# Layer 0 of a three-layer block: gates one branch later, modulation weights by GpSimd's queue, four places for gated z

## The chip, the cores and the metric

One core of a Trainium2 chip. The time is that of the device for one execution, in microseconds, as the median of three runs. The profile shown is of one further execution.

## The reference

The program computes a stack of three layers on x (1024 positions, 1024 channels, float32) with a conditioning vector c. Before each of the first two layers c gives a shift, a scale and a gate by a 1024 x 3072 matrix (the modulation); h is the normed x, scaled and shifted; the layer's output is multiplied by the gate and added to x. The change lies in layer 0, a recurrent block:

```python
proj = h @ in_w
xb, zg = proj[..., :D_RNN], proj[..., D_RNN:]
xb = causal_dwconv(xb, conv_w) + conv_b
pre = jnp.einsum('bsni,knij->kbsnj', xg, gate_w.astype(jnp.float32))   # xg: xb in 8 blocks of 128 channels
gates = jax.nn.sigmoid(pre)                                            # with gate_b
r_t, i_t = gates[0], gates[1]
log_a = -RG_C * r_t * jax.nn.softplus(-lam.astype(jnp.float32))
a_t = jnp.exp(log_a)
mult = jnp.sqrt(-jnp.expm1(2.0 * log_a))
b_t = mult * (i_t * xf)
_, hseq = lax.associative_scan(_lin_combine, (a_t, b_t), axis=1)
y = hseq.astype(h.dtype) * jax.nn.silu(zg)
return y @ out_w
```

Layer 1 is a gated delta rule in chunks, layer 2 a mix of a long convolution and a state-space model. Neither is touched.

## The kernel before, in words

Channels lie on the 128 partitions, positions along the free axis. The 1024 channels of layer 0 are worked in four groups p of 256 (two blocks e of 128). Weights come from memory in pieces of 1 MB (tile wst, two places), and are split into two float16 parts wh and wl (L104 by ScalarE, L105 by VectorE, four places); a product is three matmuls (L111 to L113), eight steps of 128 for each half of 512 positions, so 24 matmuls for one PSUM bank psmm. A group has an input branch and a z branch.

- xbranch(p): shift_proj (32 narrow matmuls for the shift's part), four projections into banks that ScalarE copies to xp (L323), the convolution of four taps (L329 by ScalarE, three L331 by VectorE for each block) into xf. Then the gates: eight float32 matmuls of xf with the gate matrices gw (L512) into banks ps_gate, sigmoids by ScalarE (L513) into gt0 and gt1, a tanh (L519) and an exponential (L522), VectorE's arithmetic (L523, L524, L527, L528) with ScalarE's L525 and square root L526 in between, and two scans (L531) that give the hidden state hs. gt0, gt1 and at have one place each. xf has one place for even and one for odd groups.
- zbranch(p): four projections, each read by ScalarE with the SiLU (L542) into zs, multiplied by the hidden state (L543), and split into two float16 parts (L123, L125) that lie over the hidden state and go into the output projection.

Beside that the modulation of later use is worked out in six parts: ada_fetch loads four tiles ast of 512 KB (four places, 24 loads in all), ada_sum multiplies them by c and adds up (L148, seven L150 for each part, VectorE), and ada_fin adds over the partitions (four transposes on TensorE, ps_ada, L186 and L187) and writes 512 numbers to memory (ada_d, L189) from GpSimd's queue. ada_step does one of each, a stage further for each part. The next stage reads ada_d back as rows GA, hn and SH.

All engines take their instructions in order. A scheduler orders them when the program is built, from the order in which the code is written and from places and data; waits between engines are semaphores. Within layer 0 the parts stand one after the other in the code at the end of the listing, with ada_step between them. SyncE's queue carries all loads of layer 0; GpSimd carries the memsets of xp's first three columns (L313), the six writes of ada_d, and later the writes of x1_d (tile x_d in the views).

Of the kernel before, what the change touches and what calls it, by code (L numbers as in the profile page):

```python
# [10 lines left out]
F32 = mybir.dt.float32  # L11
# [6 lines left out]
P = 128  # L18
D = 1024
# [5 lines left out]
WC = 256  # L25
# [3 lines left out]
def kernel(ctx, tc, ins, out):  # L29
    nc = tc.nc  # L30
    pe, dve, act, pool, sp = nc.tensor, nc.vector, nc.scalar, nc.gpsimd, nc.sync
    a = ins
# [123 lines left out]
    def ada_fetch(pl, l, part, h):  # L156

        tiles = []
        for kk in range(4):
            st = pl.tile([P, 2, 512], F32, tag="ast", name="ast", bufs=4)  # L160
            sp.dma_start(st, ada_src(l, part, h, 2 * kk, 2))
            tiles.append(st)
        return tiles, l, part, h

# [307 lines left out]
    with ExitStack() as sy:  # L472
        ypool = mkpool("y0", stack=sy)
        yT = []
        with ExitStack() as s0:
            pl = mkpool("lru", stack=s0)
            hseq = []
            PR = [P, 2, T]
            gw = []
            for g2 in range(2):  # L480
                g_ = pl.tile([P, D], F32, name=f"gw{g2}")
                sp.dma_start(g_.rearrange("p (n j) -> p n j", n=NK), a["lru_gate_w"][0, g2].rearrange("n i j -> i n j"))
                gw.append(g_)

            def xbranch(p, w):
                xf = xf0 if p == 0 else lru_xf(p, pl)
                if p > 0:
                    sb = shift_proj(w)
                for e in range(2 if p > 0 else 0):
                    xp = lru_xp(p, pl)  # L490
                    for hf in range(2):
                        lru_proj(xp, w, e, hf, sb[e])
                    lru_conv(xf[:, e], xp, 2 * p + e)
                if p == 0:
                    sb = shift_proj(w)
                    for e in range(2):
                        cs = pl.tile([P, 4], F32, tag="cs", name="cs", bufs=2)
                        dve.tensor_copy(cs[:, 0:1], col("lconv", e, 3))
                        for i in range(1, 4):
                            dve.tensor_tensor(out=cs[:, i:i + 1], in0=cs[:, i - 1:i], in1=col("lconv", e, 3 - i), op=ALU.add)  # L500
                        dve.tensor_scalar(out=cs, in0=cs, scalar1=sb[e], scalar2=None, op0=ALU.mult)
                        dve.tensor_tensor(out=xf[:, e, 0:3], in0=xf[:, e, 0:3], in1=cs[:, 0:3], op=ALU.add)
                        act.activation(xf[:, e, 3:], xf[:, e, 3:], AF.Identity, bias=cs[:, 3:4])
                tg = []
                for g2 in range(2):
                    gx = pl.tile(PR, F32, tag=f"gt{g2}", name=f"gt{g2}")
                    for e in range(2):
                        j = 2 * p + e
                        js = slice(P * j, P * (j + 1))
                        for hf in range(2):  # L510
                            ps = ps_c("ps_gate")
                            pe.matmul(ps, gw[g2][:, js], xf[:, e, HF[hf]], start=True, stop=True)  # L512
                            act.activation(gx[:, e, HF[hf]], ps, AF.Sigmoid, bias=col("lgb", j, g2))  # L513
                    tg.append(gx)
                at, it = tg
                tt = pl.tile(PR, F32, tag="at", name="at")
                for e in range(2):
                    j = 2 * p + e
                    act.activation(tt[:, e], at[:, e], AF.Tanh, scale=sp4[:, j:j + 1])  # L519
                for e in range(2):  # L520
                    j = 2 * p + e
                    act.activation(at[:, e], at[:, e], AF.Exp, scale=sp8[:, j:j + 1])  # L522
                dve.tensor_tensor(out=it, in0=it, in1=xf, op=ALU.mult)  # L523
                dve.scalar_tensor_tensor(out=at, in0=at, scalar=1.0, in1=tt, op0=ALU.add, op1=ALU.mult)  # L524
                act.activation(at, at, AF.Identity, bias=onecol)  # L525
                act.activation(tt, tt, AF.Sqrt, scale=-1.0)  # L526
                dve.scalar_tensor_tensor(out=tt, in0=at, scalar=1.0, in1=tt, op0=ALU.add, op1=ALU.mult)  # L527
                dve.tensor_tensor(out=tt, in0=tt, in1=it, op=ALU.mult)  # L528
                hs = ypool.tile(PR, F32, tag="a4", name="hs", bufs=4)
                for e in range(2):  # L530
                    dve.tensor_tensor_scan(hs[:, e], at[:, e], tt[:, e], 0.0, ALU.mult, ALU.add)  # L531
                hseq.append(hs)

            def zbranch(p, w):
                sb = shift_proj(w)
                for e in range(2):
                    yT.append([])
                    for hf in range(2):
                        ps = ps_mm()
                        mm_chT(ps, w, P * e, hTh(HF[hf]), hTl(HF[hf]))  # L540
                        zs = pl.tile([P, 512], F32, tag="zs", name="zs", bufs=2)
                        act.activation(zs, ps, AF.Silu, scale=IWS, bias=sb[e])  # L542
                        dve.tensor_tensor(out=zs, in0=zs, in1=hseq[p][:, e, HF[hf]], op=ALU.mult)  # L543

                        y = hseq[p][:, e, HF[hf]].bitcast(F16)
                        yT[-1].append((y[:, :512], y[:, 512:]))
                        split(y[:, :512], y[:, 512:], zs)

            adq = [(l, part, h) for l, part in ((0, 2), (1, 1), (1, 0)) for h in range(2)]
            adt, adp = [ada_fetch(pl, *adq.pop(0))], []  # L550

            def ada_step():
                if len(adp) == 2 or not adt:
                    ada_fin(pl, *adp.pop(0))
                if adt:
                    adp.append(ada_sum(pl, *adt.pop(0)))
                if adq:
                    adt.append(ada_fetch(pl, *adq.pop(0)))

            wx.append(load_w(a["lru_in_w"][0], 2 * WC))  # L560
            xbranch(0, wx[0])
            wz.append(load_w(a["lru_in_w"][0], D + WC))
            xbranch(1, wx[1])
            ada_step()
            wx.append(load_w(a["lru_in_w"][0], 3 * WC))
            zbranch(0, wz[0])
            ada_step()
            xbranch(2, wx[2])
            wz.append(load_w(a["lru_in_w"][0], D + 2 * WC))
            ada_step()  # L570
            zbranch(1, wz[1])
            wz.append(load_w(a["lru_in_w"][0], D + 3 * WC))
            ada_step()
            ada_step()
            xbranch(3, wx[3])
            ada_step()
            ada_step()
            zbranch(2, wz[2])
            ada_step()
            zbranch(3, wz[3])  # L580
# [972 lines left out]
```

## Time and profile before

| | |
|---|---|
| runs, median (lowest to highest) | 1833.15 us (1831.11 to 1836.46), 3 runs |
| profiled execution, its own time | 1828.97 us |
| its span | 1827.3 us |
| TensorE busy | 1741.6 us (95%) |
| VectorE busy | 1386.6 us (76%) |
| ScalarE busy | 920.1 us (50%) |
| GpSimd busy | 62.1 us (3%) |
| mean granted clock of TensorE | 0.989 |

The shares are of the whole span. Layer 0's part that the change touches lies between about 75 and 272 us; what it is worth there is read from that stretch alone. In the page a granted clock of 1.00 is TensorE's full clock. Names as psmm or ast stand for all places of a tile; L12 is line 12 of the listing.

### The profile page before, as it was taken

What the parts mean: (1) busy time and instruction counts of PE and PEld (TensorE: products, weight loads), DVE (VectorE), ACT (ScalarE), POOL (GpSimd) and SP (SyncE); (2) the same over time, 40 slices, a digit from 0 to 9 for tenths busy, and PEclk for the clock granted to TensorE, in tenths of its full rate; (3) what the DMA queues carried; (4) which work ended last, traced back from release to release, by engine and by line L of the source; (5) the groups of instructions that cost most, each with busy time, mean ns of one, the idle gap of its engine ahead of it and who ended that gap; (6) DMA issues with size and microseconds to landing.
All of it is one profiled execution on the core that took longest, in us unless ns stands there. A gap on an engine that the chain in (4) does not pass through costs nothing.

```text
span 1827.3 us, 28998 instructions
## 1 busy us (share of the span) xinstructions
PE 1741.6 (95%) x11591; PEld 1072.6 (59%) x11591; DVE 1386.6 (76%) x2429; ACT 920.1 (50%) x1642; POOL 62.1 (3%) x152
## 2 busy tenths in 40 slices
PE   4978999999899999999999998999999999999998
PEld 2433449855556656678789586555444444444487
DVE  6697767656777777887466799999999999693332
ACT  6576663256556857766443434655651221571221
POOL 0000000000000010100000300000000000000000
PEclk8999999999999999999999999999999999999999
DMA  9554345314142231444342311101321221011212
GB/s 305 164 157 140 57 72 190 104 55 132 30 120 69 62 79 33 113 130 117 128 150 82 89 50 52 53 20 51 127 81 35 70 69 64 30 41 52 81 70 93
DMA packets 165169, 165.23 MB, mean 90 GB/s; under 512 B 50094, under 2 KB 143342, under 8 KB 165034
## 3 DMA queue, kind: packets, MB, share of 16 engines
q1 hardware_dynamic: 163626, 159.17, 29.0%
q0 software_dynamic: 1408, 4.21, 0.6%
q8 instruction: 91, 1.49, 0.3%
q14 instruction: 44, 0.36, 0.1%
HBM read 139.05 MB, written 23.12 MB: 89 GB/s over the span
## 4 chain that ended last, share of the span: by engine, by line
PE 61%; DVE 25%; ACT 6%; issue 4%; DMA 3%; SPq 0%; DVEq 0%; ACTq 0%
DVE cc L1024 5%; PE psmm L113 5%; PE psmm L111 5%; PE psmm L112 5%; DVE wl L105 2%; PE ps_out L120 2%; PE ps_out L118 2%; PE ps_out L119 2%; PE ps_fin L120 2%; PE ps_fin L118 2%; PE ps_fin L119 2%; PE ps_zc L111 2%; PE ps_zc L113 2%; PE ps_zc L112 2%; ACT jk L728 1%
## 5 line engine op out<-in xcount | busy, mean ns | idle before, releaser
L111 PE MATMUL psmm<-hTh,wh 128*128 128x512 f16 x896 | 342.2, 383 | 12.7 <-ACT zs L542 10.2
L112 PE MATMUL psmm<-hTl,wh 128*128 128x512 f16 x896 | 342.8, 383 | 0.1
L113 PE MATMUL psmm<-hTh,wl 128*128 128x512 f16 x896 | 342.8, 383 | 0.0
L1024 DVE SCALAR_TENSOR_TENSOR cc<-cu,cols,cc 128x1024 f32<-128x1024 f32 (+1 forms) x270 | 301.2, 1160 | 0.9
L112 PEld LDWEIGHTS <-wh 128*128 128x128 f16 x1568 | 154.2, 98 | 183.6 <-issue 18.7
L113 PEld LDWEIGHTS <-wl 128*128 128x128 f16 x1568 | 154.2, 98 | 175.0 <-issue 8.3
L111 PEld LDWEIGHTS <-wh 128*128 128x128 f16 x1568 | 154.2, 98 | 174.4 <-issue 8.2
L105 DVE SCALAR_TENSOR_TENSOR wl<-wst,wh 128x2048 f16<-128x2048 f32 (+2 forms) x71 | 153.6, 2168 | 51.7 <-ACT wh L104 51.7
L104 ACT ACTIVATE wh<-wst 128x2048 f16<-128x2048 f32 (+2 forms) x71 | 128.4, 1811 | 94.0 <-PE ps_gs L112 27.7
L118 PE MATMUL ps_z<-wh,hTh 128*128 128x256 f16 x256 | 69.8, 273 | 0.0
L120 PE MATMUL ps_z<-wl,hTh 128*128 128x256 f16 x256 | 69.8, 273 | 0.0
L119 PE MATMUL ps_z<-wh,hTl 128*128 128x256 f16 x256 | 69.8, 273 | 0.0
L118 PE MATMUL ps_fin<-wh,merged 128*128 128x256 f16 x256 | 69.8, 273 | 0.0
L119 PE MATMUL ps_fin<-wh,merged 128*128 128x256 f16 x256 | 69.8, 273 | 0.0
L120 PE MATMUL ps_fin<-wl,merged 128*128 128x256 f16 x256 | 69.8, 273 | 0.0
L119 PE MATMUL ps_out<-wh,hs 128*128 128x256 f16 x256 | 69.7, 273 | 0.0
L118 PE MATMUL ps_out<-wh,hs 128*128 128x256 f16 x256 | 69.7, 273 | 0.0
L120 PE MATMUL ps_out<-wl,hs 128*128 128x256 f16 x256 | 69.7, 273 | 0.0
L123 ACT ACTIVATE hTh<-ps_ht 128x512 f16<-128x512 f32 x32 | 17.4, 595 | 88.0 <-PE ps_ht L271 88.0
L793 DVE TENSOR_TENSOR Tt<-Tt,tm 128x60 f32<-128x60 f32 (+24 forms) x248 | 55.9, 225 | 5.5
L791 DVE TENSOR_TENSOR tm<-Lp,Tt 128x60 f32<-128x60 f32 (+24 forms) x248 | 53.6, 216 | 5.2
L120 PE MATMUL ps_out<-wl,yo 128*128 128x256 f16 x192 | 52.3, 273 | 0.3 <-DVE wl L105 0.3
(531 smaller groups left out, 3999.9 us busy)
## 6 DMA issues: line engine op xcount, KB each, us to landing
wst<-in_w_in_dram SPq DMA_DIRECT2D x24, 1024.0 KB
wst<-in_gdn_in_w_dram SPq DMA_DIRECT2D x16, 1024.0 KB
ast<-in_ada_w_dram SPq DMA_DIRECT2D x24, 512.0 KB
xt<-in_x_dram SPq DMA_DIRECT2D x16, 512.0 KB
wst<-in_lru_in_w_dram SPq DMA_DIRECT2D x8, 1024.0 KB
sta<-in_ada_w_dram SPq DMA_DIRECT2D x8, 1024.0 KB
wst<-in_lru_out_w_dram SPq DMA_DIRECT2D x4, 1024.0 KB
x_d<-xt POOLq DMA_DIRECT2D x8, 512.0 KB, 3.0
```

What stands on the lines that cost most here:

```text
L104: act.activation(hi, st, AF.Copy, scale=WS)
L105: dve.scalar_tensor_tensor(out=lo, in0=st, scalar=WS, in1=hi, op0=ALU.mult, op1=ALU.subtract)
L111: pe.matmul(ps, wh[:, k, c0:c0 + P], ah(k), start=(k == 0), stop=False)
L112: pe.matmul(ps, wh[:, k, c0:c0 + P], al(k), start=False, stop=False)
L113: pe.matmul(ps, wl[:, k, c0:c0 + P], ah(k), start=False, stop=(k == nk - 1))
L118: pe.matmul(ps, ah(k), wh[:, k, :], start=(k == 0), stop=False)
L119: pe.matmul(ps, al(k), wh[:, k, :], start=False, stop=False)
L120: pe.matmul(ps, ah(k), wl[:, k, :], start=False, stop=(k == nk - 1))
L728: act.activation(jk, pst[:, P * c:P * (c + 1)], AF.Square, accum_out=kq[:, n, 4 * b + c:4 * b + c + 1])
L791: dve.tensor_tensor(out=tv, in0=Lp[:, j, j + 1:].unsqueeze(1).to_broadcast([P, m, n]), in1=Tt[:, :m, j:j + 1].to_broadcast([P, m, n]), op= ...
L793: dve.tensor_tensor(out=Tt[:, :m, j + 1:], in0=Tt[:, :m, j + 1:], in1=tv, op=ALU.subtract)
L1024: dve.scalar_tensor_tensor(out=acc, in0=cus[j][:, i + t0:i + t0 + n], scalar=col("cw", j, i), in1=acc, op0=ALU.mult, op1=ALU.add)
```

## The change

Three edits. The modulation loads leave from GpSimd's queue instead of SyncE's. The second half of xbranch becomes a function gates(p, xf), which is called one input branch later: x0, x1, gates 0, x2, gates 1, z0, x3, gates 2, z1, gates 3, z2, z3, with the eight calls of ada_step between them. And zs has four places instead of two. The line numbers rise by 3 from the gates on (L512 becomes L515, L542 becomes L545), and by 7 behind the order of the calls.

```diff
--- before.py
+++ after.py
@@ -158,7 +158,7 @@
         tiles = []
         for kk in range(4):
             st = pl.tile([P, 2, 512], F32, tag="ast", name="ast", bufs=4)
-            sp.dma_start(st, ada_src(l, part, h, 2 * kk, 2))
+            pool.dma_start(st, ada_src(l, part, h, 2 * kk, 2))
             tiles.append(st)
         return tiles, l, part, h
 
@@ -501,6 +501,9 @@
                         dve.tensor_scalar(out=cs, in0=cs, scalar1=sb[e], scalar2=None, op0=ALU.mult)
                         dve.tensor_tensor(out=xf[:, e, 0:3], in0=xf[:, e, 0:3], in1=cs[:, 0:3], op=ALU.add)
                         act.activation(xf[:, e, 3:], xf[:, e, 3:], AF.Identity, bias=cs[:, 3:4])
+                return xf
+
+            def gates(p, xf):
                 tg = []
                 for g2 in range(2):
                     gx = pl.tile(PR, F32, tag=f"gt{g2}", name=f"gt{g2}")
@@ -538,7 +541,7 @@
                     for hf in range(2):
                         ps = ps_mm()
                         mm_chT(ps, w, P * e, hTh(HF[hf]), hTl(HF[hf]))
-                        zs = pl.tile([P, 512], F32, tag="zs", name="zs", bufs=2)
+                        zs = pl.tile([P, 512], F32, tag="zs", name="zs", bufs=4)
                         act.activation(zs, ps, AF.Silu, scale=IWS, bias=sb[e])
                         dve.tensor_tensor(out=zs, in0=zs, in1=hseq[p][:, e, HF[hf]], op=ALU.mult)
 
@@ -558,22 +561,26 @@
                     adt.append(ada_fetch(pl, *adq.pop(0)))
 
             wx.append(load_w(a["lru_in_w"][0], 2 * WC))
-            xbranch(0, wx[0])
+            x0 = xbranch(0, wx[0])
             wz.append(load_w(a["lru_in_w"][0], D + WC))
-            xbranch(1, wx[1])
+            x1 = xbranch(1, wx[1])
+            gates(0, x0)
             ada_step()
             wx.append(load_w(a["lru_in_w"][0], 3 * WC))
+            x2 = xbranch(2, wx[2])
+            gates(1, x1)
+            ada_step()
             zbranch(0, wz[0])
+            wz.append(load_w(a["lru_in_w"][0], D + 2 * WC))
             ada_step()
-            xbranch(2, wx[2])
-            wz.append(load_w(a["lru_in_w"][0], D + 2 * WC))
+            x3 = xbranch(3, wx[3])
+            gates(2, x2)
             ada_step()
             zbranch(1, wz[1])
             wz.append(load_w(a["lru_in_w"][0], D + 3 * WC))
             ada_step()
             ada_step()
-            xbranch(3, wx[3])
-            ada_step()
+            gates(3, x3)
             ada_step()
             zbranch(2, wz[2])
             ada_step()
```

The order that the scheduler makes of it is the same on every engine from the first matmul of the output projection on. Three places in front of it, where engines wait or are waited for:

VectorE around the end of branch 1 (xf_735) before; the other names are of gates(0): gt, at and the hidden state hs_726.

```order
L524 SCALAR_TENSOR_TENSOR gt0_689<-gt0_689,at_715 128x2048
L331 SCALAR_TENSOR_TENSOR xf_735<-xp_772,cols_81,xf_735 128x1024
L105 SCALAR_TENSOR_TENSOR wl_948<-wst_945,wh_947 128x2048
L331 SCALAR_TENSOR_TENSOR xf_735<-xp_772,cols_81,xf_735 128x1024
L150 SCALAR_TENSOR_TENSOR ad_1107<-ast_939,ccol_76,ad_1107 128x512
L331 SCALAR_TENSOR_TENSOR xf_735<-xp_772,cols_81,xf_735 128x1024
L527 SCALAR_TENSOR_TENSOR at_715<-gt0_689,at_715 128x2048
L331 SCALAR_TENSOR_TENSOR xf_735<-xp_830,cols_81,xf_735 128x1024
L528 TENSOR_TENSOR at_715<-at_715,gt1_702 128x2048
L331 SCALAR_TENSOR_TENSOR xf_735<-xp_830,cols_81,xf_735 128x1024
L531 SCALAR_TENSOR_TENSOR hs_726<-gt0_689,at_715 128x1024 x2
L331 SCALAR_TENSOR_TENSOR xf_735<-xp_830,cols_81,xf_735 128x1024
```

The last step of xf stood behind the scans of gates(0).

VectorE at the same place now (xf_695 is branch 1, ad_1104 a part of the modulation).

```order
L105 SCALAR_TENSOR_TENSOR wl_908<-wst_905,wh_907 128x2048
L331 SCALAR_TENSOR_TENSOR xf_695<-xp_790,cols_81,xf_695 128x1024
L344 TENSOR_TENSOR shr_945<-shr_945 128x2
L148 TENSOR_SCALAR ad_1104<-ast_897,ccol_76 128x512
L331 SCALAR_TENSOR_TENSOR xf_695<-xp_790,cols_81,xf_695 128x1024
L150 SCALAR_TENSOR_TENSOR ad_1104<-ast_897,ccol_76,ad_1104 128x512
L331 SCALAR_TENSOR_TENSOR xf_695<-xp_790,cols_81,xf_695 128x1024
L526 TENSOR_TENSOR gt1_861<-gt1_861,xf_374 128x2048
L150 SCALAR_TENSOR_TENSOR ad_1104<-ast_899,ccol_76,ad_1104 128x512 x2
L150 SCALAR_TENSOR_TENSOR ad_1104<-ast_901,ccol_76,ad_1104 128x512
L527 SCALAR_TENSOR_TENSOR gt0_848<-gt0_848,at_874 128x2048
L150 SCALAR_TENSOR_TENSOR ad_1104<-ast_901,ccol_76,ad_1104 128x512
```

All six steps of xf (the first three stand above these rows, among sums) come ahead of the arithmetic of gates(0), whose first two operations are L526 and L527 here.

GpSimd's queue before, at the last memsets and the writes of ada_d:

```order
L313 MEMSET xp_1219 128x3
L313 MEMSET xp_1597 128x3
L189 DMA ada_d_74<-adac_75 128x4x1 x2
L313 MEMSET xp_1655 128x3
L189 DMA ada_d_74<-adac_75 128x4x1 x4
L666 MEMSET tinit_3482 128x256
L668 AFFINE_SELECT tinit_3482<-tinit_3482 32x256 x4
```

There were no loads between them.

The same now, from the write of the second part on:

```order
L189 DMA ada_d_74<-adac_75 128x4x1
L161 DMA ast_1518<-in_ada_w_dram 128x2x512
L161 DMA ast_1520<-in_ada_w_dram 128x2x512
L161 DMA ast_1522<-in_ada_w_dram 128x2x512
L161 DMA ast_1524<-in_ada_w_dram 128x2x512
L189 DMA ada_d_74<-adac_75 128x4x1
L161 DMA ast_1705<-in_ada_w_dram 128x2x512
L189 DMA ada_d_74<-adac_75 128x4x1
L161 DMA ast_1707<-in_ada_w_dram 128x2x512
L161 DMA ast_1709<-in_ada_w_dram 128x2x512
L161 DMA ast_1711<-in_ada_w_dram 128x2x512
L189 DMA ada_d_74<-adac_75 128x4x1 x2
```

The modulation loads stand between the writes in one order: ast_1705 behind the third write, the last three loads behind the fourth.

VectorE now, where the sums of the fifth and sixth part (ad_1696, ad_1721) meet the arithmetic of gates(3) (gt0_1730, gt1_1743):

```order
L150 SCALAR_TENSOR_TENSOR ad_1721<-ast_1705,ccol_76,ad_1721 128x512
L150 SCALAR_TENSOR_TENSOR ad_1696<-ast_1522,ccol_76,ad_1696 128x512
L526 TENSOR_TENSOR gt1_1743<-gt1_1743,xf_1308 128x2048
L150 SCALAR_TENSOR_TENSOR ad_1696<-ast_1522,ccol_76,ad_1696 128x512
L150 SCALAR_TENSOR_TENSOR ad_1721<-ast_1707,ccol_76,ad_1721 128x512
L150 SCALAR_TENSOR_TENSOR ad_1696<-ast_1524,ccol_76,ad_1696 128x512
L150 SCALAR_TENSOR_TENSOR ad_1721<-ast_1707,ccol_76,ad_1721 128x512
L150 SCALAR_TENSOR_TENSOR ad_1696<-ast_1524,ccol_76,ad_1696 128x512
L150 SCALAR_TENSOR_TENSOR ad_1721<-ast_1709,ccol_76,ad_1721 128x512
L527 SCALAR_TENSOR_TENSOR gt0_1730<-gt0_1730,at_1756 128x2048
L150 SCALAR_TENSOR_TENSOR ad_1721<-ast_1709,ccol_76,ad_1721 128x512
L186 TENSOR_REDUCE adac_75<-ps_ada_1770 128x4
```

L527, the first step of gates(3) that ScalarE waits for, stands behind sums that need ast_1707 and ast_1709 and the reduction of the part ps_ada_1770 stands behind them too. Before, such sums took their data from loads in SyncE's queue.

## Rows read from the trace of the kernel before

**Rows 1.** The page's first line.

```profile
span 1827.3 us, 28998 instructions
```

**Rows 2.** Windows of 20 us and one of 100: engines, TensorE clock, DMA share, GB/s.

```profile
80.00:100.00 20.00, 20.00 (x180) 10.56 (x180) 11.41 (x26) 16.80 (x23) 0.00 (x0) 1.00 1.01 332
100.00:120.00 20.00, 19.23 (x100) 8.88 (x99) 19.93 (x15) 11.79 (x11) 0.10 (x1) 1.00 0.53 182
120.00:140.00 20.00, 10.76 (x57) 4.96 (x56) 13.96 (x20) 14.53 (x17) 1.82 (x3) 0.79 0.48 92
...
180.00:280.00 100.00, 100.00 (x562) 50.46 (x561) 70.31 (x73) 68.01 (x75) 5.47 (x10) 1.00 0.38 76
```

**Rows 3.** Timeline of TensorE: start, us, instruction, idle time before it and its releaser.

```profile
111.43 1.95 PE L512 MATMUL ps_gate<-xf,gw 128*128 128x512 f32 x4 [0.77 <-DVE xf L331]
...
123.70 7.14 PE L512 MATMUL ps_gate<-xf,gw 128*128 128x512 f32 x12 [2.64 <-DVE xf L331]
...
137.87 0.58 PE L111 MATMUL psmm<-hTh,wh 128*128 128x512 f16 x1 [6.60 <-ACT zs L542]
...
142.05 0.38 PE L112 MATMUL psmm<-hTl,wh 128*128 128x512 f16 x1
142.26 0.38 PE L113 MATMUL psmm<-hTh,wl 128*128 128x512 f16 x1
...
154.04 0.38 PE L111 MATMUL psmm<-hTh,wh 128*128 128x512 f16 x1 [3.63 <-ACT zs L542]
154.26 0.38 PE L112 MATMUL psmm<-hTl,wh 128*128 128x512 f16 x1
...
171.25 1.98 PE L512 MATMUL ps_gate<-xf,gw 128*128 128x512 f32 x4 [1.50 <-DVE xf L331]
...
272.47 0.27 PE L118 MATMUL ps_out<-wh,hs 128*128 128x256 f16 x1
```

**Rows 4.** Windows of 1 us, columns as in rows 2.

```profile
128.00:129.00 1.00, 1.00 (x4) 0.42 (x3) 0.96 (x3) 0.79 (x2) 0.00 (x0) 0.83 0.86 315
...
134.00:135.00 1.00, 0.00 (x0) 0.00 (x0) 1.00 (x1) 1.00 (x2) 0.00 (x0) 1.00 0.42 27
...
138.00:139.00 1.00, 1.00 (x3) 0.29 (x2) 0.00 (x0) 0.40 (x1) 0.00 (x0) 0.50 0.95 340
...
219.00:220.00 1.00, 1.00 (x6) 0.45 (x5) 1.00 (x2) 0.00 (x0) 0.00 (x0) 1.00 0.87 36
```

**Rows 5.** Timeline of ScalarE around the first sigmoid of the second gates.

```profile
122.55 1.28 ACT L513 ACT_TABLE_LOAD   x1 [2.55 <-DVE hs L531]
```

**Rows 6.** Timeline of GpSimd, 60 to 275 us.

```profile
75.40 0.10 POOL L313 MEMSET xp<- 128x3 f32 x1 [5.01 <-DVE adac L389]
...
126.09 0.97 POOL L189 DMA_DIRECT2D ada_d<-adac  x1 [2.20 <-DVE adac L187]
```

**Rows 7.** Timeline of SyncE's queue, 60 to 275 us.

```profile
77.58 2.57 SPq L101 DMA_DIRECT2D wst<-in_lru_in_w_dram  x2
```

**Rows 8.** Lines by form, 80 to 280 us: busy us, mean ns, idle before, releasers.

```profile
L150 DVE SCALAR_TENSOR_TENSOR ad<-ast,ccol,ad 128x512 f32<-128x512 f32 x42 | 30.9, 749 | 8.4 <-DMA ast<-in_ada_w_dram 7.9
L331 DVE SCALAR_TENSOR_TENSOR xf<-xp,cols,xf 128x1024 f32<-128x1024 f32 x18 | 23.0, 1280 | 1.6 <-ACT xf L329 1.5
...
L531 DVE TENSOR_TENSOR_SCAN hs<-gt,at 128x1024 f32<-128x1024 f32 x8 | 17.9, 2276 | 0.0
...
L523 DVE TENSOR_TENSOR gt<-gt,xf 128x2048 f32<-128x2048 f32 x4 | 9.2, 2288 | 6.7 <-ACT gt L513 6.7
...
L525 ACT ACTIVATE gt<-gt,onecol 128x2048 f32<-128x2048 f32 x4 | 8.0, 1997 | 5.5 <-DVE gt L524 5.5
...
L526 ACT ACTIVATE at<-at 128x2048 f32<-128x2048 f32 x4 | 7.6, 1911 | 0.0
```

**Rows 9.** The tile ada_d, 60 to 300 us: from issue to landing.

```profile
DMA to landing us min/median/max: 8.3/9.9/12.4
```

**Rows 10.** The tile x_d, 270 to 420 us: from issue to landing.

```profile
DMA to landing us min/median/max: 2.9/3.0/5.9
```

## The prediction

> **What bounds the kernel now.** The page's first line and the windows come first [rows 1, 2]. The span is 1827.3 us; the profiled execution took 1828.97 us, the 1.7 us outside the span included. That is 4.2 us under the median of the runs shown (1833.15 us), so a gain worked out in the trace is taken off that median in the end. The change touches layer 0 between about 75 us and the output projection, whose first matmul is at 272.47 us [rows 3]; behind that every engine has the same instructions in the same order. So the question is how much earlier or later that matmul comes.
>
> The windows tell who sets it [rows 2]: TensorE is busy 20.00 of 20 us in 80:100 and 100 of 100 us in 180:280. Between them it has holes, worst in 120:140 with 10.76 us busy at a granted clock of 0.79. Its timeline shows five [rows 3]: 0.77, 2.64, 6.60, 3.63 and 1.50 us, 15.1 us together. Three wait for xf of L331, the input of the gate matmuls; two wait for zs of L542, ScalarE's reading of a z projection, that is for a free PSUM bank.
>
> Two smaller losses go with them. Behind the 6.60 us hole ten matmuls take from 137.87 to 142.05, 0.42 us each, and from there 0.21 [rows 3]: 2.0 us lost. The granted clock there is 0.50 (the level of 1.2 GHz, after the long idle) where the rest has 1.00 (2.4 GHz) [rows 4]. Behind the 3.63 us hole the next matmul follows after 0.22 us, so that one cost no clock [rows 3]. And the six gate matmuls of 123.70 take 7.14 us, while two at 111.43 take 1.95 (0.97 each), so six 5.9: 1.3 us are waits for the sigmoids. At most 15.1 + 2.0 + 1.3 = 18.4 us can go, with nothing new in their place.
>
> **What the change removes.** VectorE now finishes xf of branch 1 before the arithmetic of gates(0); before, it was spread between the steps of that arithmetic. TensorE has branch 1 done at about 95; ScalarE's copy and L329 and three L331 put xf at 100 at the earliest, and the rest of VectorE's row ahead of it makes 103.6, by adding up durations [rows 8]. TensorE reaches gates(1) only at about 123, so the holes of 111.43 and 123.70 go; that of 171.25 goes too, as gates(2) now follows all of branch 3. The zs holes go because z0 and z1 now come one input branch further behind the gates whose result they multiply, and four zs places let ScalarE empty four z banks before VectorE has multiplied one. I remove all five, the slow clock and the 1.3. Of the activation-table loads of 1.28 us each [rows 5], about a dozen go; outside the holes ScalarE was not TensorE's limit, so I count nothing more.
>
> **What it adds on TensorE.** Four terms.
> (1) The first four modulation loads (2 MB) leave GpSimd right behind the memset of 75.40 [rows 6], ahead of the weights and gate matrices that SyncE issues from 77.58 [rows 7]. The DMA engines then run full, 332 GB/s in 80:100 [rows 2]: 2 MB ahead put the later ones up to 6.3 us back, less the 2.1 us that they start sooner. A projection in front of gates(0) covers some of it. Bounds 0 and 4.2; I take 1.5, the nearer to the dense row of 80:100.
> (2) In gates(1) the places gt and at are single, so its first sigmoid waits for the scans of gates(0). VectorE from 103.6: four operations at 2.29 (9.2), six sums at 0.7 (4.2), two L331 at 1.2 (2.4), two scans (4.5), and a wait at the square root, where ScalarE needs 2.0 + 1.28 + 1.91 = 5.2 us and VectorE has 2.1 us of sums meanwhile: 3.1 [rows 8]. That ends at 127.0. A table load of 1.28 stands behind the scan as it does at 122.55 [rows 5], then a sigmoid of 0.6: 128.9. TensorE needs the bank for the fourth gate matmul at about 126.3: 2.6 us, between 0 and 5.
> (3) The same wait in gates(3), near 207: 1.3, between 0 and 2.6.
> (4) Gate matmuls paced by sigmoids in the other gates blocks, between 0 (no hole behind 171.25 until 272) and three times 1.3: I take 0.8.
> Sum 6.2, so 18.4 - 6.2 = 12.2 us of gain, if the modulation loads land in time.
>
> **The queue.** The six results of the modulation parts (ada_d, 2 KB written in elements of 4 bytes) and the 24 loads now share GpSimd's one order. Before, such a write took 8.3 to 12.4 us to land, median 9.9 [rows 9], and while it ran SyncE's loads nearly stood: the rate fell from 315 GB/s to 27 after the write of 126.09 [rows 6], was 340 again at 138:139, and 36 at 219:220 after the third write [rows 4]. The low spell after 126.09 is some 8 us long. In the new order the writes of the third and fourth part stand on both sides of ast_1705 and ahead of ast_1707, 1709 and 1711, and VectorE's row has the sums of these ahead of L524 of gates(3) (L527 in the new numbering). I place these two writes at 206.4 and 209.6, from the same adding up. Then ast_1705 is usable at 206.4 + 9.9 + 1.4 (512 KB at full rate) = 217.7, ast_1707 one more spell of about 7 later, 224.5. Five sums (3.5) put L524 at 228.0; L524 2.3, ScalarE's 2.0 + 1.28 + 1.91, a table load 1.28 and the zs 0.6 [rows 5, 8] free the PSUM bank at 237.4. TensorE would want it for the last projection of z2 at 232. So 5.2 us are lost there, and the gain is 12.2 - 5.2 = 7.0 us: 1828.97 - 7.0 = 1822.0 on the profiled execution and 1833.15 - 7.0 = 1826.1 on the median; I say 1826. A slow clock behind that hole, as behind the 6.60 us one, would leave 5.0 of it.
>
> In the Trainium skill, the page "DMA: Bandwidth & Descriptors", section "Issuing engines are not separate DMA queues", says that transfers started by another engine run on the same 16 DMA engines, and that only the sequencer's time is saved. By it the queue's change gives nothing by itself; the sum above has no gain for it either, and the falling rate of rows 4 agrees that the queues are not independent.
>
> Other edits at nothing: GpSimd's memsets of xp now stand behind loads that wait for VectorE (xp_1006 behind the seventh load). The sums waited for are over more than 5 us before ScalarE writes that xp; without this cover a branch comes late by up to the wait for one sum and its load, some 3 us. SyncE's weight loads no longer stand behind modulation loads and come earlier than they are needed. The next stage's loads of ada_d need the sixth write, which now comes with about 10 us of cover.
>
> **Rivals.**
> A. The writes do not hold the loads: 12.2 us of gain, 1821 by the median (1814.8 at the ceiling of 18.4). For it: a write of x_d, 512 KB and also from GpSimd, lands in 3.0 us [rows 10], so that queue is not slow by itself. Against it: the rates of rows 4.
> B. No change: both writes take the longest landing in turn, 206.4 + 12.4 + 12.4 + 1.4 = 232.6 for ast_1707, so 13.3 us are lost instead of 5.2, and 1834 comes out by the median. For it: the two stand in one queue, with a load between. Against it: in the old order, with the same writes, VectorE waited 7.9 us for ast at L150 in all [rows 8].
> C. Slower: GpSimd's queue serves one 512 KB load at a time. From 75.5, with four writes at 9.9 and 24 loads of t each, the last is in at 115.1 + 24 t; about 6 us of VectorE and ScalarE and five projections of 5.2 follow. That meets the old 272.47 at t = 5.2. At the longest landing of x_d, 5.9 [rows 10], it gives 289, 16 us lost, 1849; at the median of 3.0 all of it is hidden, which is the row against it.
> The Trainium skill, "SBUF — State Buffer", section "Who interferes with whom", says that a transfer started from GpSimd is starved while VectorE runs in a two-port mode. No row here shows that; by its rule it would be rival C.
>
> **How the numbers follow.** A measurement of this kernel tells about 0.3% (5.5 us) from no change. The forecast (gain 5 to 9) has 0.40, of which 0.04 falls under 5.5; A 0.22; B 0.23; C and what else loses 0.15. So faster 0.36 + 0.22 = 0.58, same 0.04 + 0.23 = 0.27, slower 0.15. The forecast's own range is 1824 to 1828. From 1815 (A at its ceiling) to 1838 (B, and the spread of 3 us that the runs of before have above their median) leaves out about 0.15, most of it C.
>
> **What would show it.** Right: no wait of TensorE for zs between 125 and 180 and none for xf; a hole of 2 to 3 us near 126 ended by ScalarE; another of 4 to 7 us between 220 and 240 behind a late ast; the first output matmul near 265.5. Wrong: that second hole missing (A, output near 260) or over 12 us (B); VectorE waiting for ast from the first parts on (C). The forecast fails as well if the first gate matmul is more than 4 us late for its matrices, or a hole appears that no term names.

## The result and the profile after

The changed kernel took 1842.33 us (median of 4 runs, 1841.51 to 1843.95); the kernel before, in the runs beside it, 1832.13 us. The ratio is 1.0056, 95% interval 1.0039 to 1.0072: slower by 10.2 us, where 1826 us was forecast. The profiled execution took 1842.77 us with a span of 1840.6 us. The first output matmul comes at 280.05 us instead of 272.47 [rows 3], 7.6 us late; the other 5.7 us by which the two spans differ arise behind it, and are taken up at the end.

Windows of 20 us of the changed kernel, with the columns of [rows 2] ("..." stands for lines not shown, here and below):

```profile
80.00:100.00 20.00, 16.44 (x165) 8.60 (x164) 13.01 (x28) 9.71 (x14) 2.27 (x4) 0.83 1.04 352
100.00:120.00 20.00, 20.00 (x80) 8.75 (x79) 15.83 (x15) 17.25 (x19) 3.71 (x6) 1.00 0.51 143
120.00:140.00 20.00, 17.17 (x75) 7.61 (x74) 18.16 (x11) 13.06 (x14) 0.10 (x1) 0.91 0.27 81
...
200.00:220.00 20.00, 18.00 (x79) 8.14 (x76) 17.66 (x21) 14.50 (x17) 2.46 (x4) 1.00 0.28 95
220.00:240.00 20.00, 11.97 (x39) 5.12 (x39) 8.35 (x9) 9.39 (x12) 3.40 (x5) 0.84 0.83 127
240.00:260.00 20.00, 16.91 (x132) 9.08 (x133) 17.24 (x18) 9.55 (x11) 0.78 (x1) 0.82 0.51 111
```

The holes of 100:180 are gone (140:160 and 160:180 have 20.00 us busy each) but for 120:140, which has 17.17 us busy where it had 10.76. In their place TensorE stands in 80:100 and in 200:260, stretches that were full before, and the granted clock is 0.82 to 0.84 in three of the windows.

The timeline of TensorE, in answer to [rows 3]; all stretches that it waited from 80 us on, and the first output matmul:

```profile
90.62 0.16 PE L340 MATMUL ps_sh<-shl,wh 128*128 128x2 f16 x1 [2.43 <-ACT shr L343]
...
92.34 2.04 PE L515 MATMUL ps_gate<-xf,gw 128*128 128x512 f32 x2 [1.13 <-DMA gw<-in_lru_gate_w_dram]
...
135.15 2.07 PE L515 MATMUL ps_gate<-xf,gw 128*128 128x512 f32 x2 [2.83 <-ACT gt L516]
...
218.63 1.12 PE L515 MATMUL ps_gate<-xf,gw 128*128 128x512 f32 x2 [1.97 <-ACT gt L516]
...
243.09 1.08 PE L185 MATMUL ps_ada<-ident,ad 128*128 128x128 f32 x4 [11.02 <-DVE ad L150]
...
280.05 0.27 PE L118 MATMUL ps_out<-wh,hs 128*128 128x256 f16 x1
```

None of the five old waits is there. The new ones are 2.43 + 1.13 before gates(0), 2.83 in gates(1), 1.97 in gates(3) and 11.02 at the reduction of the fifth modulation part: 19.4 us against 15.1.

Windows of 1 us, in answer to [rows 4].

```profile
94.00:95.00 1.00, 1.00 (x3) 0.29 (x2) 1.00 (x2) 1.00 (x1) 0.62 (x1) 0.50 1.08 386
...
222.00:223.00 1.00, 1.00 (x3) 0.48 (x2) 1.00 (x2) 0.79 (x2) 0.00 (x0) 0.50 0.93 20
...
226.00:227.00 1.00, 1.00 (x7) 0.45 (x5) 0.00 (x0) 1.00 (x2) 0.00 (x0) 1.00 0.36 16
...
239.00:240.00 1.00, 0.00 (x0) 0.00 (x0) 0.00 (x0) 0.00 (x0) 0.00 (x0) 0.50 0.98 397
...
245.00:246.00 1.00, 1.00 (x4) 0.30 (x2) 1.00 (x2) 0.33 (x2) 0.00 (x0) 0.50 0.04 8
```

Clock 0.50 stands in 94:95 behind the first wait, in 222:223 behind that of gates(3), and at 245 behind the longest. The rate is 20 and 16 GB/s in the spell of the two writes, and 397 in 239:240.

ScalarE, in answer to [rows 5]: the split of the weights that branch 1's shift needs, and the first sigmoid of gates(1).

```profile
86.53 1.91 ACT L104 ACTIVATE wh<-wst 128x2048 f16<-128x2048 f32 x1 [3.62 <-DMA wst<-in_lru_in_w_dram]
...
133.12 1.28 ACT L516 ACT_TABLE_LOAD   x1 [2.95 <-DVE hs L534]
```

The weights were waited for until 86.53; behind that split stands the copy L343 (at 90.42), which frees TensorE's bank for the next shift. The table load of gates(1) waits for the scan as its counterpart did.

GpSimd's queue, in answer to [rows 6]:

```profile
75.57 3.11 POOL L161 DMA_DIRECT2D ast<-in_ada_w_dram  x4 [0.47 <-issue]
...
216.70 0.78 POOL L189 DMA_DIRECT2D ada_d<-adac  x1 [13.88 <-DVE adac L187]
219.77 0.71 POOL L161 DMA_DIRECT2D ast<-in_ada_w_dram  x1 [2.29 <-DVE adac L187]
220.47 0.78 POOL L189 DMA_DIRECT2D ada_d<-adac  x1
232.76 1.43 POOL L161 DMA_DIRECT2D ast<-in_ada_w_dram  x2 [11.52 <-DVE ad L150]
```

The four loads leave ahead of SyncE's weights, which follow at 77.18 (77.58 in [rows 7]). Later a write, a load (ast_1705), a write; the next loads leave only at 232.76, when VectorE has freed their places. The prediction had put the two writes at 206.4 and 209.6; they left at 216.70 and 220.47.

VectorE's two waits for those loads:

```profile
231.32 0.49 DVE L148 TENSOR_SCALAR ad<-ast,ccol 128x512 f32<-128x512 f32 x1 [8.31 <-DMA ast<-in_ada_w_dram]
...
240.20 1.41 DVE L150 SCALAR_TENSOR_TENSOR ad<-ast,ccol,ad 128x512 f32<-128x512 f32 x2 [3.55 <-DMA ast<-in_ada_w_dram]
```

ast_1705 took 11.5 us from issue to first use, ast_1707 then 7.4. Between 75 and 300 us VectorE waited for ast nowhere else.

One line by form, in answer to [rows 8], 80 to 290 us, and the issues and landing times of ast, in answer to the x_d of [rows 10]:

```profile
L331 DVE SCALAR_TENSOR_TENSOR xf<-xp,cols,xf 128x1024 f32<-128x1024 f32 x18 | 23.0, 1279 | 0.2
```

```profile
L161 POOL DMA_DIRECT2D ast<-in_ada_w_dram x24: 707/724/933, 75.6 to 237.0; - x24
...
DMA to landing us min/median/max: 4.1/5.8/13.3
```

VectorE's wait for xf is down from 1.6 to 0.2 us, and an operation takes what it took. A load takes GpSimd 0.72 us to issue and 5.8 us in the median to land, up to 13.3.

### The profile page after: what moved, and what is told of

Its sections match the earlier page's. It is cut to its first block, busy times and chain, and to the rows that moved or that the text cites. A ratio compares the mean times of both kernels' runs of the same rounds, so it can differ in the third digit from the quotient of the medians.

```text
span 1840.6 us, 29002 instructions
## 1 busy us (share of the span) xinstructions
PE 1747.5 (95%) x11591; PEld 1075.3 (58%) x11591; DVE 1386.8 (75%) x2429; ACT 908.4 (49%) x1633; POOL 80.2 (4%) x176
## 4 chain that ended last, share of the span: by engine, by line
PE 59%; DVE 26%; ACT 7%; issue 4%; DMA 3%; SPq 0%; DVEq 0%; POOL 0%; ACTq 0%; POOLq 0%
DVE cc L1031 5%; PE psmm L113 4%; PE psmm L112 4%; PE psmm L111 4%; DVE wl L105 3%; PE ps_out L120 2%; PE ps_out L118 2%; PE ps_out L119 2%; PE ps_fin L120 2%; PE ps_fin L118 2%; PE ps_fin L119 2%; PE ps_zc L112 2%; PE ps_zc L111 2%; PE ps_zc L113 1%; ACT jk L735 1%
```

## The experiments

Twelve kernels ran, in three groups. The kernel before, run beside each group, took 1834.54 us (e1 to e4), 1836.05 us (e5 to e8) and 1835.91 us (e9 to e12), so kernels of different groups are compared by their ratios to it. Two theories stood against each other at first: that GpSimd's queue costs the time (Q), or that the new order does (O).

**The change without the queue** (e1_order_zs4_sync).

```diff
-            pool.dma_start(st, ada_src(l, part, h, 2 * kk, 2))
+            sp.dma_start(st, ada_src(l, part, h, 2 * kk, 2))
```

> The changed kernel with the modulation loads back on SyncE's queue; gates one branch later and four zs places stay. Theory Q (GpSimd's queue costs it: four loads ahead of the gate matrices, and writes of ada_d between the last loads): the stall of 3.6 us before gates(0) with its slow clock of some 3 us and the hole of 11 us at ps_ada with its slow clock of 2.5 us go, about 20 us of 1842, so 1820 to 1825 us, ratio to before 0.994 to 0.997. Theory O (the new order itself costs it, by the waits in gates(1) and gates(3) on single places): the holes of 2.8 and 2.0 us and their slow clock stay and nothing is gained, 1830 to 1840 us, ratio 1.000 or above.

1831.4 us (1828.29 to 1837.63 in twelve runs), ratio to before 0.9986 (0.9970 to 1.0001): no slower than the kernel before, and by the ratios 13 us under the changed kernel. So the queue's edit is what made the change slower; the waits tell how much of it is understood. Its TensorE timeline:

```profile
129.79 1.22 PE L515 MATMUL ps_gate<-xf,gw 128*128 128x512 f32 x1 [2.67 <-ACT gt L516]
...
238.34 0.87 PE L185 MATMUL ps_ada<-ident,ad 128*128 128x128 f32 x3 [11.93 <-DVE ad L150]
...
275.89 0.27 PE L118 MATMUL ps_out<-wh,hs 128*128 128x256 f16 x1
```

The wait before gates(0) is gone, so the early loads made it. But the longest one is there with 11.93 us although the loads are on SyncE's queue: GpSimd's one order is not what makes it. Both theories fall in their simple form: Q had the long wait gone and 1820 to 1825 us, O had nothing gained by putting the loads back. VectorE's waits show that the same two loads are late:

```profile
226.94 0.49 DVE L148 TENSOR_SCALAR ad<-ast,ccol 128x512 f32<-128x512 f32 x1 [9.05 <-DMA ast<-in_ada_w_dram]
...
236.78 2.08 DVE L150 SCALAR_TENSOR_TENSOR ad<-ast,ccol,ad 128x512 f32<-128x512 f32 x3 [3.72 <-DMA ast<-in_ada_w_dram]
```

**The queue alone** (e2_queue_only): the kernel before with the line of e1 the other way round.

```diff
-            sp.dma_start(st, ada_src(l, part, h, 2 * kk, 2))
+            pool.dma_start(st, ada_src(l, part, h, 2 * kk, 2))
```

> The kernel before with the modulation loads on GpSimd's queue and nothing else. Theory Q: slower than before, 1838 to 1848 us (ratio 1.003 to 1.009), with a stall before the first gate matmul and sums of VectorE late behind a write of ada_d. Theory O: within 0.2% of before, as transfers hide.

1857.03 us, ratio 1.0121 (1.0101 to 1.0141): slower by more than theory Q said. The stall at the start is there, and long waits around the modulation that the kernel before has not:

```profile
91.06 0.16 PE L340 MATMUL ps_sh<-shl,wh 128*128 128x2 f16 x1 [2.54 <-ACT shr L343]
...
236.36 0.88 PE L185 MATMUL ps_ada<-ident,ad 128*128 128x128 f32 x3 [8.28 <-DVE ad L150]
...
244.15 1.22 PE L512 MATMUL ps_gate<-xf,gw 128*128 128x512 f32 x1 [4.57 <-DVE xf L331]
...
295.69 0.27 PE L118 MATMUL ps_out<-wh,hs 128*128 128x256 f16 x1
```

**Four zs places alone** (e3_zs4_only), in zbranch of the kernel before.

```diff
-                        zs = pl.tile([P, 512], F32, tag="zs", name="zs", bufs=2)
+                        zs = pl.tile([P, 512], F32, tag="zs", name="zs", bufs=4)
```

> The kernel before with four zs places and nothing else; TensorE's order is that of before. Of the two zs holes the second (3.63 us) waits for a place of zs and goes; the first (6.60 us) is ScalarE's order and stays. Theory Q and theory O both say 0 to 4 us faster, ratio 0.998 to 1.000. If the first hole also goes (the prediction's reading, that four places empty the banks), 8 to 12 us faster, 0.994.

1834.84 us, ratio 0.9992 (0.9974 to 1.0009): no change. The hole of 6.60 us stays as it was, so it is not a place; ScalarE works through it without a pause, on the gates' operations that stand ahead of the first zs in its order. Of the 3.63 us, 2.27 stay, and the last wait for xf grows from 1.50 to 4.84 us.

```profile
138.06 0.59 PE L111 MATMUL psmm<-hTh,wh 128*128 128x512 f16 x1 [6.60 <-ACT zs L542]
...
152.94 0.38 PE L111 MATMUL psmm<-hTh,wh 128*128 128x512 f16 x1 [2.27 <-ACT zs L542]
```

**The order alone** (e4_order_only): the changed kernel with both other edits undone.

```diff
-            pool.dma_start(st, ada_src(l, part, h, 2 * kk, 2))
+            sp.dma_start(st, ada_src(l, part, h, 2 * kk, 2))
...
-                        zs = pl.tile([P, 512], F32, tag="zs", name="zs", bufs=4)
+                        zs = pl.tile([P, 512], F32, tag="zs", name="zs", bufs=2)
```

> Gates one input branch later and nothing else: modulation loads on SyncE's queue, two zs places. Theory Q: faster than before, 1820 to 1828 us (ratio 0.994 to 0.998), a little above the same with four zs places. Theory O: 1832 us or more, ratio 1.000 to 1.006.

1838.23 us, ratio 1.0021 (1.0008 to 1.0035). The two old zs waits are gone with two places as well, so the order alone removes them. The long wait is there too, and with two zs places another one behind it:

```profile
236.77 0.45 PE L185 MATMUL ps_ada<-ident,ad 128*128 128x128 f32 x1 [9.03 <-DVE ad L150]
...
255.29 0.58 PE L111 MATMUL psmm<-hTh,wh 128*128 128x512 f16 x1 [3.50 <-ACT zs L545]
```

So it comes with the order. It could be the slow writes (W), which the prediction had named, on whatever queue the loads are, or that the places for the loads free too late (P).

**Writes in larger pieces** (e5_pieces16): e1 with a write of 128 pieces of 16 B instead of 512 of 4 B. It leaves out putting the numbers back in order where they are read, so later stages take them permuted; otherwise the instructions are those of e1.

```diff
-        pool.dma_start(ada_d[l, c0:c0 + 512].rearrange("(k p) -> p k", p=P), o)
+        pool.dma_start(ada_d[l, c0:c0 + 512].rearrange("(p k) -> p k", p=P), o)
```

> Gates later, four zs places, loads on SyncE (the kernel of e1_order_zs4_sync) with the ada_d results written in 128 pieces of 16 B instead of 512 of 4 B (the numbers then stand in another order in ada_d, so the result is not the reference's). TensorE's order is the same. Theory W (a write in small pieces holds the transfers of all queues; that makes the hole of 11.9 us at ps_ada): the write lands in 3 to 5 us instead of 10.6, ast_1705 in 4 to 6 instead of 12.5, the hole shrinks to 2 to 5 us, and the time falls by 8 to 11 us to a ratio of about 0.993 to before. Theory P (the loads are only issued late, because the new order frees the four ast places late): the hole stays at 9 to 12 us and the ratio at 0.998.

1820.06 us (1816.05 to 1823.96), ratio 0.9917 (0.9900 to 0.9934), 11 us under e1 by the medians and 13 by the ratios. TensorE's order is the same; its wait goes from 11.93 to 0.53 us, and the output comes 13.7 us earlier:

```profile
226.25 0.41 PE L185 MATMUL ps_ada<-ident,ad 128*128 128x128 f32 x2 [0.53 <-DVE ad L150]
...
262.21 0.27 PE L118 MATMUL ps_out<-wh,hs 128*128 128x256 f16 x1
```

From issue to landing, the tile ada_d in e1 and then in this kernel (the kernel before: [rows 9]):

```profile
DMA to landing us min/median/max: 9.1/10.6/16.9
```

```profile
DMA to landing us min/median/max: 1.7/2.7/4.6
```

The order of the loads and their places is that of e1, so W holds, and P, by which that order alone makes the loads late, falls. Places do pass the delay on: the last three loads leave at 219.11 instead of 228.11, because VectorE is not kept waiting for ast_1705 and so frees their places sooner.

**Results as rows** (e6_rows): e1 with a matmul by a column of ones in place of four transposes and a reduction.

```diff
         for kk in range(4):
-            pe.transpose(pst[:, P * kk:P * (kk + 1)], acc[:, P * kk:P * (kk + 1)], ident)
-        dve.tensor_reduce(out=o, in_=pst.rearrange("p (k c) -> p k c", k=4), op=ALU.add, axis=mybir.AxisListType.X)
...
+            dve.scalar_tensor_tensor(out=acc[:, ks], in0=ident, scalar=cols[:, 4 * h + kk, j:j + 1], in1=acc[:, ks],
+                                     op0=ALU.mult, op1=ALU.add)
...
+        pe.matmul(psr[0:1, :], onecol, acc, start=True, stop=True)
...
+        dve.tensor_copy(row, psr[0:1, :])
...
+        pool.dma_start(ada_d[l:l + 1, c0:c0 + 512], row)
```

> As e1_order_zs4_sync, with each ada_d result made as a row (one matmul with a column of ones, bias added before it) and written in pieces of 128 B. TensorE pays 0.86 us for each of six parts instead of 0.5 to 0.6, VectorE 0.7 us more. Theory W: the write lands in 2 to 3 us, the hole at ps_ada is 0 to 4 us, ratio to before 0.991 to 0.995. Theory P: hole 9 to 12 us, ratio 0.998 to 1.000.

1834.55 us, ratio 0.9993 (0.9982 to 1.0005), where 0.991 to 0.995 was expected: a miss. No wait of VectorE for ast is left, so W holds here too, but other waits took the place, the longest for the small operations that add the bias:

```profile
249.79 1.01 PE L188 MATMUL ps_ada<-ad,onecol 128*1 128x512 f32 x1 [3.60 <-DVE ad L185]
...
272.85 0.27 PE L118 MATMUL ps_out<-wh,hs 128*128 128x256 f16 x1
```

**The change with those rows** (e7_queue_rows): the changed kernel with the edit of e6.

> The changed kernel (loads on GpSimd's queue) with the rows of e6_rows. What is left between the two is the queue alone without the slow writes. Theory W with the loads ahead of the gate matrices as the second cause: the stall of 3.6 us before gates(0) and its slow clock stay, so 6 to 8 us above e6_rows, ratio to before 0.995 to 0.999. If loads from GpSimd are slow by themselves: more than 10 us above e6_rows, with VectorE waiting for ast.

1845.9 us, ratio 1.0057 (1.0043 to 1.0071), 11 us above e6: by the time the second of the two cases that were named, but without its sign. ast lands in 4.8 us in the median and 8.4 at most without the slow writes, and VectorE waited only 1.8 us for it, so the loads are not slow by themselves; the stall at the start (2.60 + 1.28 us) is a part of the 11.

**The first four loads behind the gate matrices** (e8_first_sync): the changed kernel with SyncE's queue for these four alone (ada_fetch takes the queue as q).

```diff
-            pool.dma_start(st, ada_src(l, part, h, 2 * kk, 2))
+            (q or pool).dma_start(st, ada_src(l, part, h, 2 * kk, 2))
...
-            adt, adp = [ada_fetch(pl, *adq.pop(0))], []
+            adt, adp = [ada_fetch(pl, *adq.pop(0), q=sp)], []
```

> The changed kernel with the first four of the 24 modulation loads on SyncE's queue again, behind the gate matrices; the other 20 stay on GpSimd. If the order of these four against the weights makes the stall before gates(0) (3.6 us and some 3 us of slow clock): both go, 6 to 7 us faster than the changed kernel, 1835 to 1837 us, ratio to before 1.001 to 1.003. If the queue itself does it: no change against it, ratio 1.0056.

1838.29 us, ratio 1.0011 (0.9998 to 1.0024): under the changed kernel by 4 us by the medians and 8 by the ratios, where 6 to 7 were expected. The stall before gates(0) is gone and the first wait is that of gates(1); the long one stays. The output starts at 274.97, 5.1 us earlier than in the changed kernel.

```profile
128.85 0.70 PE L515 MATMUL ps_gate<-xf,gw 128*128 128x512 f32 x1 [2.73 <-ACT gt L516]
...
236.89 0.87 PE L185 MATMUL ps_ada<-ident,ad 128*128 128x128 f32 x3 [12.38 <-DVE ad L150]
```

**16 B pieces, read back rightly** (e9_best): e1 with the pieces, and VectorE reading the permuted rows GA, SC and SH by a strided view.

```diff
-        c0 = D * part + 512 * h
-        pool.dma_start(ada_d[l, c0:c0 + 512].rearrange("(k p) -> p k", p=P), o)
+        dst = ada_d[l, D * part:D * (part + 1)].rearrange("(p k) -> p k", k=NK)
+        pool.dma_start(dst[:, 4 * h:4 * h + 4], o)
...
-            dve.tensor_tensor(out=tmp, in0=ps, in1=GA[:, 512 * hf:512 * (hf + 1)], op=ALU.mult)
+            dve.tensor_tensor(out=nat(tmp), in0=nat(ps), in1=perm(GA)[:, 4 * hf:4 * hf + 4], op=ALU.mult)
```

> Gates later, four zs places, loads on SyncE, and ada_d written in 128 pieces of 16 B, now read back rightly: the rows stay permuted in memory and VectorE reads them through a strided view. Theory W: as e5_pieces16, ratio to before 0.990 to 0.994, first output matmul near 262 us. If a strided read is slower for VectorE (0.6 us more for each of some 50 operations behind the output projections), 0.995 to 1.000.

1824.52 us, ratio 0.9940 (0.9925 to 0.9955): faster than both kernels. The output starts at 260.44, as in e5 or earlier:

```profile
260.44 0.27 PE L118 MATMUL ps_out<-wh,hs 128*128 128x256 f16 x1
```

Besides the place of each piece in memory, it differs from e5 in the strided reads alone, so the 4 us between the two are put down to these. Lines of VectorE in the output projection of this kernel, and of the kernel before:

```profile
L301 DVE TENSOR_TENSOR rtmp<-ps_out,GA 128x512 f32<-128x512 f32 x16 | 17.2, 1077 | 10.4 <-PE ps_out L120 10.4
L272 DVE TENSOR_TENSOR hn<-hn,SH 128x1024 f32<-128x1024 f32 x8 | 16.2, 2022 | 0.2
```

```profile
L295 DVE TENSOR_TENSOR rtmp<-ps_out,GA 128x512 f32<-128x512 f32 x16 | 11.0, 690 | 20.3 <-PE ps_out L120 20.3
...
L266 DVE TENSOR_TENSOR hn<-hn,SH 128x1024 f32<-128x1024 f32 x8 | 9.8, 1225 | 0.2
```

**16 B pieces in the kernel before** (e10_before_pieces): the kernel before with e9's writes and strided reads.

> The kernel before with the writes in 16 B pieces and nothing else. If the slow writes cost only in the new order (the writes there stand ahead of the last loads): 0 to 3 us faster, ratio 0.998 to 1.000, TensorE's zs and xf holes as they were. If they cost in any order, in layer 1 as well: 5 to 10 us faster, 0.994 to 0.997.

1832.47 us, ratio 0.9981 (0.9971 to 0.9992), its strided reads paid for. The zs hole of 6.6 us and the first two xf holes stand as before, the last is 0.46 instead of 1.50, the one of 3.63 is gone, and the output starts at 266.89, 5.6 us earlier. So the slow writes cost something in the old order too, but less than in the new one, where shortening them brought the output 13.7 us forward.

**16 B pieces in the changed kernel** (e11_after_pieces): the changed kernel with e9's writes and strided reads.

> The changed kernel with the writes in 16 B pieces: loads on GpSimd's queue as in the change. Theory W with the early loads as the second cause: 6 to 8 us above e9_best, by the stall of 3.6 us before gates(0) and its slow clock, ratio to before 0.994 to 0.998, no hole over 2 us at ps_ada. If GpSimd's queue has a cost of its own: more than 10 us above e9_best, ratio above 0.998.

1841.45 us, ratio 1.0030 (1.0015 to 1.0046), 17 us above e9 where 6 to 8 were expected. That is the second of the cases named: GpSimd's queue has a cost of its own. The stall at the start is there (2.42 and 1.15 us), and 3.23 us are left at the reduction:

```profile
235.79 0.41 PE L185 MATMUL ps_ada<-ident,ad 128*128 128x128 f32 x2 [3.23 <-DVE ad L150]
```

Its first output matmul is at 272.79 us, 12.4 behind e9. One window from 80 us to the output tells what these 12.4 are, in this kernel and then in e9:

```profile
80.00:272.00 192.00, 180.23 (x972) 84.13 (x972) 145.49 (x160) 119.35 (x137) 20.15 (x34) 0.96 0.41 131
```

```profile
80.00:260.00 180.00, 173.05 (x972) 81.81 (x971) 145.72 (x160) 118.63 (x137) 6.22 (x14) 1.00 0.44 142
```

TensorE has 972 matmul records in both. It stands 11.8 us instead of 7.0, and it is busy 7.2 us longer, at a granted clock of 0.96 in the mean instead of 1.00: most of this cost of the queue is slow clock behind the waits. The rest of the 17 us is behind the output's start.

**Two places for gt0** (e12_gt2): e9, with three zs and three ast places to make room (these two lines are not shown).

```diff
-                    gx = pl.tile(PR, F32, tag=f"gt{g2}", name=f"gt{g2}")
+                    gx = pl.tile(PR, F32, tag=f"gt{g2}", name=f"gt{g2}", bufs=2 - g2)
```

> As e9_best with two places for gt0 (paid for with three zs and three ast places instead of four). If the holes of 2.7 and 2.0 us in gates(1) and gates(3) come from gt0's single place: both go with their slow clock, 4 to 8 us under e9_best, ratio to before 0.986 to 0.990. If the tanh's single place at, or the three ast places, take over: within 2 us of e9_best.

1825.2 us, ratio 0.9943 (0.9928 to 0.9958): as e9. The wait of gates(1) went, that of gates(3) stayed at 1.95 us, and one of 1.92 us for zs is new, so its reason is not tested cleanly.

## Why the prediction was wrong, step by step

The step that failed is the size of what the change adds: 11.4 us were put on TensorE up to the output projection (6.2 for the four terms, 5.2 for the late loads), and 26.8 came, 19.4 of waits and 7.4 of work lost at the slow clock (granted clock 0.50) behind them. The largest part is the late loads: 5.2 us at the bank of z2 in the forecast, 11.02 and 2.0 of slow clock at the reduction in the trace. The slow clock behind new waits had no place in the sum.

- **The gain was right.** All five waits went. Only the reason given for the zs holes was half wrong: e3 shows that places had no part in the one of 6.60 us, and e4 that the order removes both without them.
- **A reading that hid the price.** The prediction took 1.3 us of the six gate matmuls of 123.70 for waits for the sigmoids. The trace of before has the slow clock there, behind the wait of 2.64 us:

```profile
125.00:126.00 1.00, 1.00 (x2) 0.34 (x1) 1.00 (x4) 0.68 (x2) 0.00 (x0) 0.50 0.00 0
```

TensorE is busy all through, at 0.50 until 128, and loses 1.7 us; ScalarE waited for TensorE there (0.71 us at 126.39), not the other way round. So a wait of 2.64 us with slow clock behind it stood in that trace, and terms 1 to 3, waits of that size, were priced without it. Term 4, 0.8 us, was sized by the 1.3 and has no counterpart: the other terms already add up to the delay.

- **Term 1, the loads ahead of the gate matrices: 1.5 us forecast, bounds 0 to 4.2.** Measured 2.43 + 1.13 = 3.6 us of wait, and the clock then stood at 0.50 from 92.34 to 97, 2.3 us of work lost: 5.9, above the bounds. The cover that was named, a projection in front, was not enough, because the weights of branch 1 came late as well. e8 takes the wait away with that one edit.
- **Terms 2 and 3, the waits in gates(1) and gates(3): 2.6 and 1.3 forecast.** Measured 2.83 and 1.97, so their size was about right, and ended by ScalarE as said. But 1.4 and 1.7 us of slow clock came with them, which the sum did not have.
- **The late loads: 5.2 us forecast, with 2.0 of slow clock as an afterthought.** Measured 11.02, and 2.0 of slow clock. The place and the cause were as forecast: VectorE late for ast_1705 and ast_1707 behind two writes, and e5 removes it by shortening the writes alone. The loads took 11.5 and 7.4 us where 11.3 and 6.8 were put. Two things were off. Between the first of the two writes and the use of ast_1707 lie 23.5 us instead of 18.1, because ast_1705 itself left 3.1 us behind that write and ast_1707 only 1.4 us after ast_1705 was there, for its place. And the loss was reckoned at the PSUM bank of z2 (237.4 - 232, which is 5.4), with no term for a wait at the transposes of the reduction; TensorE reached these first, at 232.07, and there the 11.02 us lie. That the shared queue was the reason, as the prediction's heading had it, is refuted for this wait by e1.
- **The sum.** Before, the waits were 15.1 us and the slow clock 2.0 + 1.7: 18.8. Now they are 26.8, which is 8.0 more; the output was 7.6 us late. It came at 280.05 where 265.5 was forecast.
- **The queue's own price.** The prediction gave GpSimd's queue no price beyond these terms. Four pairs differ in the queue alone: the changed kernel against e1, e2 against the kernel before, e7 against e6, e11 against e9. By the ratios the loads on GpSimd cost 13, 22, 12 and 17 us. Shown of it are the early stall with its slow clock (5.9 us in the changed kernel) and, in e11 against e9, 12.4 us up to the output. The rest is open.
- **The rivals.** A is refuted: the loads are held. B came nearest: it had 13.3 us lost by the late loads, and 11.02 + 2.0 were. What stood against it, VectorE's 7.9 us of waits for ast at L150 before, left out another 8.3 us at L148. C, the slower one, has the sign but not its mechanism: VectorE did not wait for ast from the first parts on, and without slow writes no load from GpSimd took over 8.4 us (e7), though four leave together at 75.85. The Trainium skill, "SBUF — State Buffer", section "Who interferes with whom", would have transfers from GpSimd starved while VectorE is in a two-port mode. The issues took 0.71 to 0.93 us all through, so the trace shows no starving; that VectorE was in such a mode meanwhile no row shows. The Trainium skill, "DMA: Bandwidth & Descriptors", section "Issuing engines are not separate DMA queues", has all transfers on the same 16 DMA engines. The trace agrees: in 80:100 their share is 1.04 with 352 GB/s, where it was 1.01 with 332 [rows 2], so the other queue gave little more bandwidth and changed who came first.
- **What stays open.** Behind the first output matmul the changed kernel lost another 5.7 us against the profiled execution of before. That execution lay 3.2 us under the median of its runs and the changed kernel's 0.4 above its own, so some 3.6 of the 5.7 may be scatter. Some of it recurs: VectorE's waits for GB at the start of layer 1 add up to 6.6 to 7.9 us in the nine kernels with these loads on SyncE (6.6 before), and to 8.9 to 10.0 in the five with loads on GpSimd (9.3 in the changed kernel). Its line of the waits in the changed kernel, 370 to 560 us:

```profile
DVE E L714 <- DMA GB<-gb_d: 9.3, 2, 5.5
```

Why loads on GpSimd's queue in layer 0 should go with a later read some 150 us on was not found, nor the last 5 or so of the 17 us between e11 and e9.

## What to carry to other kernels

A small write in tiny pieces is not small: ask how many pieces it has and who loads while it runs, on any queue. When an order is changed to remove waits, follow the transfers that stood far from such a write before and stand next to it now. And price every new wait of TensorE with the slow clock that can follow it: here it added more than a third to the waits. A stretch of matmuls that takes long is compared with the granted clock of its own microseconds before it is put down to another engine. And when several edits go in together, the pairs that differ in one of them show which one costs: here the one that moved nothing but the queue.

## What the runs showed of the hardware

- 512 numbers in 4 B pieces took 8.3 to 12.4 us to land in the kernel before and 9.1 to 16.9 in e1, and left the other queues 16 to 36 GB/s in the windows shown; in 16 B pieces they took 1.7 to 4.6 us (e5). That edit alone was worth 11 to 13 us (e5 against e1).
- A wait of 2.7 us of TensorE was followed by the slow clock in the profile of e1 (four matmuls at about 0.43 us, granted clock 0.50 in 130:133) and not in that of e9 at the same place (1.00). In the changed kernel a wait of 1.97 us was followed by 0.50 in 220:223. What decides it was not found.
- A read of float32 at a stride of 32 B took VectorE 1077 instead of 690 ns for 512 elements, and 2022 instead of 1225 for 1024 (e9 against the kernel before).
- 24 loads of 512 KB from GpSimd's queue instead of SyncE's cost 12 to 22 us in four pairs of kernels that differ in nothing else, though no load by itself was slow without the writes (e7: 4.8 us in the median).
